# Six of the queries' column tiles as three pairs by seven products, the pair operands of h made while v is multiplied, and attention's result by way of DRAM

## The chip, the cores and the metric

The kernel runs on one core of one Trainium2 chip. The metric is the device time of that core in microseconds, lower is better. PE is TensorE's matmul queue, PEld its weight loads; DVE is VectorE, ACT is ScalarE, POOL is GpSimd and SP is SyncE, which issues most DMAs.

## What is computed

One trunk layer of a decoder, for 512 prompt tokens and 64 sample tokens together (576 columns), with a width of 1024. Cut from the reference:

```python
h = _rmsnorm(x, norm1_g) * (1.0 + sc1) + sh1          # sc1, sh1, g1, ...: silu(c) @ w_ada + b_ada
proj = h @ w_in                                       # 1024 x 6656
b_gate, c_gate, xa, q, k, v, ga, gb = jnp.split(proj, cuts, axis=-1)
uc, new_conv = _causal_conv(c_gate * xa, conv_buf, conv_w)
ya = (b_gate * uc) @ w_conv_out
o, k_state, v_state = attend(q, k, v, sinks)          # window 128, 16 heads of 64, 4 kv heads
yb = o @ w_attn_out
mixed = jax.nn.sigmoid(ga) * ya + jax.nn.sigmoid(gb) * yb
x = x + g1 * (mixed @ w_mix_out)
# then a ConvFFN (w_up, depthwise convolution, GELU gate, w_down) in the same manner, and a final norm
```

The results are wanted in float32. Every matrix product is made from high and low parts: three passes, weights high by activations high, high by low, low by high.

## The kernel before, in words

Activations lie transposed: eight row blocks of 128 channels by 576 tokens, each as a high and a low tile. A weight block of 1024 rows by 128 columns is loaded by SP (`raw`), its high part made by ACT (`whi`), its low part by DVE (`wlo`). There are four buffers for `raw` and five each for `whi` and `wlo`.

`product(w, xs)` makes one column tile of 128: eight k-steps of three passes in two column groups (256 and 320), 48 matmuls. `pair_product` makes two column tiles by seven products of half the size (Strassen's manner): each of seven parts is four k-steps of three passes of 288 columns, 12 matmuls, 84 in all. Its weights are sums of the two tiles' blocks (`pair_weights`: A, B and C of 1024 columns, D of 512, made by four DVE sums of 512 and then split); its activations are sums and differences of blocks of h (`PairOperands`: four DVE sums of 288 columns for each of four block pairs, a high part on ACT, a low part on DVE). The seven parts go into three PSUM banks X, Y and Z. Between parts ACT subtracts one bank from another (`minus`) or copies one; the outputs are read by the functions `out_a0` to `out_b1`.

In order of the program: norm and modulation up to about 50 us; v as five products of another shape (`for i in range(5)`, 53 to 67 us); the first two tiles of the queries (67 to 73); then the loop `for at, m in enumerate(PLAIN)` with six turns, to about 228. Each turn makes column tile m of c and of x of the convolution branch by two plain products. Turns 1, 2 and 3 also make a part of the keys (`key_parts`) and two tiles of the queries (`queries`), by plain products. In turns 4 and 5 of before, the pair operands of h are made. Then come 14 pair jobs with w_in, 4 pair jobs with w_conv_out (the last ends at about 450), 8 plain products with w_attn_out (450 to 497), the mix, and the ConvFFN.

`queries` splits each tile into q and a low part and copies half of it between partitions by POOL-issued DMAs (`q<-low`). Attention's scores, softmax and values run as a generator beside all this: `tick()`, called after each k-step, advances it by a rate, `filler[1]`. After attention the same generator runs `modulation`, which loads tiles of w_ada (`ada<-in_w_ada` on SP) and multiplies them (`side_by_side`, L1234). Attention's result o is kept in two tiles `ot` of tag "oh" until `part_o` splits it during the last pair jobs.

PE's order is the program's from attention on, and the jobs also fix that of ACT and DVE. In the PLAIN loop a scheduler sets the order on ACT, DVE, POOL and SP. The helpers record their operations at one line, L112 (before) and L114 (after), so tiles are told apart by name.

Of the kernel before, what the change touches and what calls it, by code (L numbers as in the profile page):

```python
# [16 lines left out]
P = 128  # L17
# [13 lines left out]
ROWS_AHEAD = 5  # L31
PLAIN = (0, 1, 2, 4, 5, 6)
Q_TICKS = 8
CACHE_AT = 15, 16
EPS = 1e-6
NEG = -1e33
# [36 lines left out]
def step_kernel(ctx: ExitStack, tc: tile.TileContext, ins: dict, outs: list):  # L73
# [169 lines left out]
    class PairOperands:  # L243
# [47 lines left out]
        def all(self):  # L291
# [2 lines left out]
            self.low()  # L294
            self.n3()

    class BesideOperands:


# [91 lines left out]
            self.low(self.x1, self.r1)  # L391
            self.low(self.n4, self.r0[:, :HT])

    def pair_weights(ra, rb, moved=""):
# [22 lines left out]
        def s3_slots():  # L417
            return slot("wh", F32R, [P, 4, P]), slot("wl", F32R, [P, 4, P])
# [30 lines left out]
    def pair_product(w, x, steps, out_a0, out_a1, out_b0, out_b1):  # L449

        X, Z = (aux()[:, :HT] for _ in range(2))
        Y = halves(mmps())[1][:, :HT]
        p5 = slot("p5")[:, :HT]

        def part(bank, wn, xn_, more=True):

            (hi, lo), xs = w[wn], x[xn_]
            for k in range(4):  # L460
                xh, xl = xs[k]
                passes = (hi(k), xh), (hi(k), xl), (lo(k), xh)
                for n, (wt, xx) in enumerate(passes):
# [345 lines left out]
    for j in (2, 0, 1):  # L809
# [2 lines left out]
            nc.scalar.activation(t[:, c0:c1], x, AF.Copy, scale=HD**-0.5 if j == 2 else 1.0)  # L812
        kT.append(t)
    q0 = kT.pop(0)

    def state_load(src, n):

# [25 lines left out]
    def tok_cols(t, i):  # L843

        at = i * P if i < 4 else NT - P
        return t[:, at : at + P]

    for i in range(5):
        ps = aux()
        for k in range(NK):  # L850
            whi, wlo = (x[:, k % 4, :] for x in wv[k // 4])
# [32 lines left out]
            nc.gpsimd.dma_start(x[other].bitcast(F32), x[mine].bitcast(F32))  # L884
        KS[hd] = kh, kl

    def queries(t, ps=None):

        scale = HD**-0.5 if ps is None else 1.0
# [32 lines left out]
        nc.gpsimd.dma_start(snk, ins["attn_sinks"][0, :].partition_broadcast(P))  # L922
    )
    key_parts(0)
    queries(0, q0)
    queries(1)
    con = slot("con", shape=[P, 520])
    nc.sync.dma_start(con[:, 0:256], ins["consts"][:, CND : CND + 256])
    nd = con[:, 0:256]
# [36 lines left out]


    pinned.append(pe)
    ot = [wp.tile([P, 4, NT], F32, tag="oh", name=nm("o"), bufs=2) for _ in range(2)]

    def softmax_steps(s, n, sinks, nsinks, w):

# [83 lines left out]
    def decode_values(q, s, cV):  # L1056
# [9 lines left out]
            pt.append(t)  # L1066
            yield False
        yield False
        c = slice(512 + 32 * q, 512 + 32 * q + 32)
        for j in range(2):  # L1070
            O = aux()
            parts = [(vt(4)[:, j * P : j * P + P], pt[1], slice(0, P))]
# [9 lines left out]
            oX = slot("oX", shape=[P, 2, 32])  # L1082
            for hf in range(2):
                src = O[HALF[hf], :P].rearrange("p (b x g t) -> p x g b t", b=4, x=2, g=2)
                dst = ot[j][:, 2 * hf : 2 * hf + 2, c]
# [44 lines left out]

    def prompt_values(parts):
        O = aux()
        for u, (hd, i, pts) in enumerate(parts):
            nkt, c = len(pts), slice(256 * u, 256 * u + 256)
            for n in range(2 * nkt):
# [7 lines left out]
                if u + n:  # L1143
                    tc.keep_in_program_order(done)
        for u, (hd, i, pts) in enumerate(parts):
            nc.scalar.copy(
                ot[hd // 2][:, 2 * (hd % 2) : 2 * (hd % 2) + 2, i * P : i * P + P],
                O[:, 256 * u : 256 * u + 256].rearrange("p (g c) -> p g c", g=2),
            )

    def attention():
        units = [(hd, i) for hd in range(4) for i in range(4)]
# [17 lines left out]
        for n in range(3):  # L1170
# [3 lines left out]
            if before is not None:  # L1174
                yield from before
            before = decode_values(n, s, more)

    sto = cp.tile([P, 18 * NF], F32, tag="sto", name="sto")

# [98 lines left out]

    def beside_conv():
        yield from attention()  # L1280
        filler[1] = 40 / 84
        yield from modulation(2048)
        yield True

    fill(beside_conv(), .3)
    sg_dram = dp.tile([2, NK, P, NT], F32, name="sg_dram")
    ycv, gcv, made, made_g = {}, {}, {}, {}
    wco, wao = ins["w_conv_out"][0], ins["w_attn_out"][0]

    class Job:  # L1290
# [7 lines left out]
            self.raws = [load_w(kpm(self.mat, self.c + e), NK) for e in (0, self.apart)]  # L1298

        def prepare(self, moved="", late=False):  # L1300
            self.w, t = pair_weights(*self.raws, moved=moved)
# [122 lines left out]
    hp = [PairOperands(h, kp, made, xn) for kp in range(4)]  # L1424

    def operands(kp):
        hp[kp].sums()
        hp[kp].high()
        hp[kp].low()

    for at, m in enumerate(PLAIN):
        if at in (4, 5):
# [6 lines left out]
                    ),  # L1439
                )  # L1440
            )
        if 1 <= at <= 3:
            key_parts(at)
            for t in (2 * at, 2 * at + 1):
                queries(t)
        w = weights(kpm(w_in, 1024 + m * P), NK)
        if at in (4, 5):
            operands(2 * at - 8)
        if at == 5 and filler:
            filler[1] = .4  # L1450
        ps = product(w, h)
# [6 lines left out]
        c_sb = slot("c")  # L1458
        nc.scalar.copy(c_sb, ps)
        w = weights(kpm(w_in, 2048 + m * P), NK)  # L1460
        if at in (4, 5):
            operands(2 * at - 7)
        steps = {}
        if at == len(PLAIN) - 1:
            jobs[0].load()
        if at == len(PLAIN) - 1:
# [24 lines left out]
    def g_list(names):  # L1491
        return [g_at(int(n[0]), n[1:]) for n in names.split()]

    jobs[0].before = {2: [op.n3 for op in hp]}
    jobs[1].before = {3: [lambda: inner[6]()]}
    jobs[7].before = {2: [lambda: inner[3]()]}
    jobs[8].before = {2: [lambda: inner[7]()]}
# [8 lines left out]
        },  # L1506
        12: {0: "1third_low 3third 2third_low", 2: "3third_low"},
    }
    for n, at in plan.items():
        jobs[n + 2].after = {p: g_list(names) for p, names in at.items()}  # L1510
    for n in range(4):
        if n:
            jobs[n_conv + n].before = {
                1: [lambda n=n: late[2 * n - 2]()], 2: [lambda n=n: late[2 * n - 1]()],
            }
    jobs[-1].after = {
        2: [lambda: part_o(2)], 3: [lambda: part_o(3)],
        4: [lambda: w_next.update({1: split_w(w_raw)})], 5: [lambda: part_o(4)], 6: [lambda: part_o(6)],
        7: [lambda: part_o(8)],
    }  # L1520

    def part_o(n):
        for k in range(len(o), n):
            o.append(split_slot(ot[k // 4][:, k % 4, :], "o"))

    for n, job in enumerate(jobs):
        if n + 1 == len(jobs):
# [711 lines left out]
```

## Time and profile before

| | before |
|---|---|
| time, median of 3 runs | 962.78 us (962.68 to 963.0) |
| profiled execution | 963.13 us, of which span 961.0 |
| PE busy | 946.4 us, 98% of the span, 7326 matmuls |
| DVE, ACT, POOL busy | 711.9, 539.1, 132.3 us |
| moved by DMA | 144.08 MB, mean 150 GB/s |

The profile is of one execution; its busy times are shares of the span. Windows of the trace give the same for a stretch of time; groups of instructions give a count, the busy time and the mean of one; the waits give what an engine waited for, in total, how often, and the longest.

### The profile page before, as it was taken

How to read it: one execution, taken by the hardware profiler on the slowest of the kernel's cores; microseconds unless marked ns; L12 is line 12 of the kernel's file. 1: busy time of each engine (PE TensorE's matmuls, PEld its weight loads, DVE VectorE, ACT ScalarE, POOL GpSimd, SP SyncE). 2: the span in 40 equal slices, each digit the busy share in tenths (PEclk: the TensorE clock that was granted, in tenths of full speed). 3: DMA queues.
4: the chain of work that ended last, by engine and by line, in shares of the span. 5: the costliest groups of instructions: out<-in, count | busy, mean ns of one | idle time of the engine just before them, and what ended most of it. 6: DMA issues, size and time to landing. Idle time of an engine off the chain costs nothing.

```text
span 961.0 us, 18726 instructions
## 1 busy us (share of the span) xinstructions
PE 946.4 (98%) x7326; PEld 912.7 (95%) x7326; DVE 711.9 (74%) x1331; ACT 539.1 (56%) x1020; POOL 132.3 (14%) x309
## 2 busy tenths in 40 slices
PE   6999999999999999999999999999999999999997
PEld 5799999998999989999889999999999999999997
DVE  4656787697966767776677688995559998868874
ACT  5454665556665446875335567563226565546664
POOL 2122112201211011210001131100000001101110
PEclk9999999999999999999999999999999999999999
DMA  9985332423655767899885732332323333328542
GB/s 275 330 255 147 90 86 71 131 90 96 155 147 178 244 219 199 219 250 285 283 291 119 174 97 66 89 109 67 107 88 92 89 89 101 92 72 172 138 95 99
DMA packets 182650, 144.08 MB, mean 150 GB/s; under 512 B 7688, under 2 KB 162124, under 8 KB 182274
## 3 DMA queue, kind: packets, MB, share of 16 engines
q1 hardware_dynamic: 172546, 111.72, 38.8%
q0 software_dynamic: 9872, 30.92, 14.0%
q8 instruction: 57, 0.93, 0.4%
q14 instruction: 31, 0.25, 0.1%
q10 hardware_dynamic: 144, 0.26, 0.1%
HBM read 113.89 MB, written 12.07 MB: 131 GB/s over the span
## 4 chain that ended last, share of the span: by engine, by line
PE 95%; DMA 3%; SPq 1%; ACT 0%; DVE 0%; issue 0%; DVEq 0%
PE mm L112 55%; PE aux L112 37%; PE aux L1234 2%; DMA ad<-in_w_ada 1%; PE aux L1137 1%; DMA raw<-in_w_in 1%; SPq L497 1%; DMA q<-low 0%; ACT whi L112 0%; ACT wlo L112 0%; DVE cs L504 0%; ACT hh L112 0%; DVE hl L112 0%; DVE yo L112 0%; ACT acc L112 0%
## 5 line engine op out<-in xcount | busy, mean ns | idle before, releaser
L112 ACT ACTIVATE whi<-raw 128x1024 fp32r<-128x1024 f32 (+3 forms) x183 | 185.6, 1022 | 108.7 <-PE mm L112 51.9
L112 DVE TENSOR_TENSOR wlo<-raw,whi 128x1024 fp32r<-128x1024 f32 (+2 forms) x160 | 188.8, 1186 | 49.0 <-ACT whi L112 48.1
L112 PE MATMUL mm<-hh,whi 128*128 128x256 f32 x336 | 74.3, 302 | 0.5 <-ACT hh L112 0.5
L112 PE MATMUL mm<-hh,wlo 128*128 128x256 f32 x336 | 71.7, 295 | 0.0
L112 PE MATMUL mm<-hl,whi 128*128 128x256 f32 x336 | 70.8, 295 | 0.1
L112 PE MATMUL aux<-2h,whi 128*128 128x288 f32 (+2 forms) x232 | 68.6, 296 | 0.0
L112 PE MATMUL aux<-2l,whi 128*128 128x288 f32 (+2 forms) x232 | 68.5, 295 | 0.0
L112 PE MATMUL aux<-2h,wlo 128*128 128x288 f32 (+2 forms) x232 | 68.3, 294 | 0.0
L112 DVE TENSOR_TENSOR raw<-raw 128x512 f32<-128x512 f32 x82 | 57.5, 701 | 2.6
L112 PEld LDWEIGHTS mm<-hh,whi 128*128 128x128 f32 x336 | 55.1, 189 | 1.8 <-ACT hh L112 1.0
L112 PEld LDWEIGHTS mm<-hl,whi 128*128 128x128 f32 x336 | 55.6, 188 | 0.7 <-DVE hl L112 0.5
L112 PEld LDWEIGHTS mm<-hh,wlo 128*128 128x128 f32 x336 | 56.2, 188 | 0.0
L112 PE MATMUL aux<-hh,whi 128*128 128x288 f32 (+2 forms) x184 | 54.0, 301 | 0.0
L112 PE MATMUL aux<-hl,whi 128*128 128x288 f32 (+2 forms) x184 | 53.0, 295 | 0.0
L112 PE MATMUL aux<-hh,wlo 128*128 128x288 f32 (+2 forms) x184 | 52.9, 295 | 0.0
L112 PE MATMUL mm<-th,whi 128*128 128x288 f32 x164 | 49.2, 300 | 0.0
L112 PE MATMUL mm<-nh,whi 128*128 128x288 f32 x164 | 49.0, 299 | 0.0
L112 PE MATMUL mm<-th,wlo 128*128 128x288 f32 x164 | 48.6, 296 | 0.0
L112 PE MATMUL aux<-th,wlo 128*128 128x288 f32 x164 | 48.5, 296 | 0.0
L112 PE MATMUL aux<-th,whi 128*128 128x288 f32 x164 | 48.5, 296 | 0.0
L112 PE MATMUL mm<-nh,wlo 128*128 128x288 f32 x164 | 48.5, 296 | 0.0
L112 PE MATMUL mm<-nl,whi 128*128 128x288 f32 x164 | 48.4, 295 | 0.0
(374 smaller groups left out, 3012.3 us busy)
## 6 DMA issues: line engine op xcount, KB each, us to landing
raw<-in_w_in SPq DMA_DIRECT2D x52, 512.0 KB, 5.0
raw<-in_w_up SPq DMA_DIRECT2D x44, 512.0 KB, 3.8
ada<-in_w_ada SPq DMA_DIRECT2D x64, 256.0 KB, 5.5
wlo<-raw POOLq DMA_DIRECT2D x17, 512.0 KB, 4.6
ad<-in_w_ada SPq DMA_DIRECT2D x32, 256.0 KB, 6.6
raw<-in_w_down SPq DMA_DIRECT2D x16, 512.0 KB, 4.2
sg_dram<-sg POOLq DMA_DIRECT2D x16, 288.0 KB, 4.9
gt<-sg_dram SPq DMA_DIRECT2D x16, 288.0 KB, 6.0
```

What stands on the lines that cost most here:

```text
L112: done = getattr(self.engine, name)(*args, **kwargs)
L497: return tc.keep_in_program_order(nc.sync.dma_start(dst, src))
L1137: done = nc.tensor.matmul(O[HALF[par], c], vt(i - nkt + 1 + kt)[:, hd * 64 : hd * 64 + 64], pts[kt][:, par * 256 : par * 256 + 256], start ...
L1234: done = nc.tensor.matmul(ps[32 * j : 32 * j + 32, :], cT[:, k, :], cols[k][j], start=(k == 1), stop=(k == NK - 2),)
```

## The change

At turns 1, 2 and 3 of the PLAIN loop (`Q_PAIRS`), the two tiles of the queries are made by one `pair_product` instead of two plain products. Its weights are prepared during the plain product ahead of it (`q_job`), D in a `whi` and a `wlo` tile instead of slots of their own (`narrow=False`). X and Y lie in the banks of the plain products and Z in a small one (`apart=True`). The result goes to SBUF (`qt`), and `queries` reads it there.

The pair operands of h are made during v's product (`EarlyOperands`, one block pair at each of i = 1 to 4) and not at turns 4 and 5; n3, which was made in jobs[0], is made with them. They take the two "oh" tiles. So o lies in slots `ot`, is written to `o_dram` by POOL-issued DMAs (eight of 128x512 and one for the 64 sample columns), and is read back by `load_o` on SP, eight loads of 128x576, in the last two pair jobs.

Besides: the copies of o from PSUM are 32 of 128 columns and not 16 of 256; the mask constants `nd` lie in a part of V; the table load of Exp stands earlier; the filler's rate is .2 in a pair and .32 after it; the rate of the modulation goes from 40/84 to 40/100; and some of the last operands ("third") for w_conv_out's jobs stand one part earlier.

```diff
+Q_PAIRS = (1,2,3,)
+OPS_AT = 1, 2, 3, 4
...
+    class EarlyOperands(PairOperands):
+        def high(self):
+            made, (h0, l0), (h1, l1) = self.made, *self.x
+            if "t" not in made:
+                made["t"] = [wp.tile([P, 4, NT], F32R, tag="oh", name=nm("t"), bufs=2) for _ in range(2)]
+            self.th, self.tl = (x[:, self.kp, :] for x in made["t"])
+            act.activation(self.th, self.t, AF.Copy)
...
+            act.activation(self.nh, self.r[0][:, a], AF.Copy)
+            act.activation(self.n3h, self.r[0][:, b], AF.Copy)
...
+        def low(self):
+            for lo, src, hi in (
+                (self.tl, self.t, self.th), (self.nl, self.r[0][:, :HT], self.nh),
+                (self.n3l, self.r[0][:, HT:], self.n3h),
+            ):
+                dve.tensor_tensor(out=lo, in0=src, in1=hi.bitcast(F32), op=ALU.subtract)
...
-        X, Z = (aux()[:, :HT] for _ in range(2))
-        Y = halves(mmps())[1][:, :HT]
+        X, Y = (halves(mmps())[1][:, :HT] if apart or n else aux()[:, :HT] for n in range(2))
+        Z = aux()[:, :HT]
...
+    act.activation(first, q0[:, 0:1], AF.Exp, scale=0.0)
...
     for i in range(5):
+        if i in OPS_AT:
+            EarlyOperands(h, OPS_AT.index(i), made, xn).all_early()
...
-    ot = [wp.tile([P, 4, NT], F32, tag="oh", name=nm("o"), bufs=2) for _ in range(2)]
+    ot = []
+    o_dram = dp.tile([NK, P, NT], F32, name="o_dram")
+    od = []
...
-            nc.scalar.copy(
-                ot[hd // 2][:, 2 * (hd % 2) : 2 * (hd % 2) + 2, i * P : i * P + P],
-                O[:, 256 * u : 256 * u + 256].rearrange("p (g c) -> p g c", g=2),
-            )
+            for g in range(2):
+                at = 256 * u + P * g
+                t = ot[2 * hd + g]
+                nc.scalar.copy(t[:, i * P : i * P + P], O[:, at : at + P])
+                if i == 3:
+                    nc.gpsimd.dma_start(o_dram[2 * hd + g, :, 0:512], t[:, 0:512])
...
-        filler[1] = 40 / 84
+        filler[1] = 40/100
...
     for at, m in enumerate(PLAIN):
+        w = weights(kpm(w_in, 1024 + m * P), NK)
         if 1 <= at <= 3:
             key_parts(at)
-            for t in (2 * at, 2 * at + 1):
-                queries(t)
-        w = weights(kpm(w_in, 1024 + m * P), NK)
-        if at in (4, 5):
-            operands(2 * at - 8)
+            if at in Q_PAIRS:
+                qt = [slot("qt") for _ in range(2)]
+                filler[1] = .2
+                pair_product(q_job.w, made["op"], {}, *copy_outs(qt), True)
+                filler[1] = .32
+            for n in range(2):
+                queries(2 * at + n, qt[n] if at in Q_PAIRS else None)
...
         w = weights(kpm(w_in, 2048 + m * P), NK)
-        if at in (4, 5):
-            operands(2 * at - 7)
         steps = {}
+        if at + 1 in Q_PAIRS:
+            q_job = Job(w_in, Q0 + (2 * at + 2) * P, None, None)
+            q_job.load()
+            fs = [f for x in q_job.prepare("").values() for f in x]
+            for k, n in [(0, 2), (1, 1), (2, 1), (3, 1), (4, 2), (5, 1), (6, 1), (7, 1)]:
+                steps[k], fs = fs[:n], fs[n:]
...
-    jobs[0].before = {2: [op.n3 for op in hp]}
...
+    jobs[-2].after = {4: [lambda: load_o(2)], 6: [lambda: load_o(4)]}
     jobs[-1].after = {
-        2: [lambda: part_o(2)], 3: [lambda: part_o(3)],
+        0: [lambda: load_o(5)], 1: [lambda: load_o(6)],
+        2: [lambda: part_o(2), lambda: load_o(7)], 3: [lambda: part_o(3), lambda: load_o(8)],
...
+    def load_o(n):
+        for k in range(len(o) + len(o_raw), n):
+            o_raw.append(slot("ot"))
+            nc.sync.dma_start(o_raw[-1], o_dram[k])
```

On ACT, at the start of turn 1, before has the weights' high parts and the queries' copies one after the other (`whi` a weight block, `y` the convolution, `kh` the keys, `s` an exp of the softmax):

```order
L112 ACTIVATE whi_1588<-raw_1586 128x1024
L112 ACTIVATE y_1096<-pad_1089,parT 128x592
L112 ACTIVATE kh_1100<-kT_663 64x512
L112 ACTIVATE whi_1702<-raw_1700 128x1024
L896 ACTIVATE q_1230<-mm_1112 64x512
L896 ACTIVATE q_1231<-mm_1112 64x512
L984 ACTIVATE s_1119,den_1139<-s_1119,nmx_1135 128x256 x2
```

The same place on ACT in after:

```order
L114 ACTIVATE whi_1180<-raw_1178 128x1024
L114 ACTIVATE y_1174<-pad_1167,parT 128x592
L114 ACTIVATE kh_1184<-kT_663 64x512
L1029 ACTIVATE s_1092,den_1112<-s_1092,nmx_1108 128x128 x2
L1029 ACTIVATE s_1093,den_1112<-s_1093,nmx_1108 128x128 x2
L114 ACTIVATE mm_1193<-mm_1192 128x288
L1035 ACTIVATE es_1113<-es_1113 128x4
L114 COPY p_1195<-aux_1194 128x288
L114 ACTIVATE aux_1194<-mm_1193 128x288
```

The pair's steps between its parts (`mm_1193<-mm_1192`, the copy `p_1195`, `aux_1194<-mm_1193`) now stand in ACT's queue behind a plain weight's high part, y, kh and the exps.

On SP, around the last pair job, before has the loads of w_attn_out, of gates (`gt`) and of w_ada:

```order
L151 DMA raw_5625<-in_w_attn_out 128x8x128
L1365 DMA gt_5627<-sg_dram 128x576
L1365 DMA gt_5629<-sg_dram 128x576
L1250 DMA ada_5641<-in_w_ada 128x512
L1250 DMA ada_5657<-in_w_ada 128x512
L151 DMA raw_5791<-in_w_attn_out 128x8x128
```

The same place on SP in after:

```order
L153 DMA raw_5700<-in_w_attn_out 128x8x128
L1585 DMA ot_5675<-o_dram 128x576
L1585 DMA ot_5677<-o_dram 128x576
L1417 DMA gt_5702<-sg_dram 128x576
L1417 DMA gt_5704<-sg_dram 128x576
L1585 DMA ot_5712<-o_dram 128x576
L1302 DMA ada_5718<-in_w_ada 128x512
L1585 DMA ot_5731<-o_dram 128x576
L1302 DMA ada_5736<-in_w_ada 128x512
L153 DMA raw_5874<-in_w_attn_out 128x8x128
```

The loads of o now stand between those of the weights, the gates and w_ada.

On POOL, before has the queries' copies of a head group in a row:

```order
L903 DMA q_1690<-low_1689 64x512
L903 DMA q_1691<-low_1689 64x512
L903 DMA q_1822<-low_1821 64x512
L903 DMA q_1823<-low_1821 64x512
L914 DMA qS_830<-qX_831 64x4x16 x2
```

After has writes of o among them:

```order
L947 DMA q_1832<-low_1831 64x512
L947 DMA q_1833<-low_1831 64x512
L947 DMA q_1843<-low_1842 64x512
L1200 DMA o_dram<-ot_1587 128x512
L1200 DMA o_dram<-ot_1588 128x512
L947 DMA q_1844<-low_1842 64x512
```

Two writes of o stand ahead of the group's last copy.

More of the change, by code (lines that the diff above doesn't have):

```diff
@@ L295, in all, with all_early @@
             self.n3()
+    class EarlyOperands(PairOperands):
[5 more added lines that the diff above has]
+            act.activation(self.th, self.t, AF.Copy)
+            if self.kp % 2 == 0:
+                for n in ("n4", "n3"):
+                    made[n] = slot(n + "h", F32R), slot(n + "l", F32R)
+            a, b = slice(0, HT), slice(HT, NT)
+            at = (a, b)[self.kp % 2]
+            nh, nl = made["n4"]
+            self.nh, self.nl = nh[:, at], nl[:, at]
+            self.n3h, self.n3l = (x[:, at] for x in made["n3"])
+            act.activation(self.nh, self.r[0][:, a], AF.Copy)
+            act.activation(self.n3h, self.r[0][:, b], AF.Copy)
+            for name, hi, lo, c in (
+                ("x00", h0, l0, a), ("n3", *made["n3"], at), ("x10", h1, l1, a), ("x11", h1, l1, b),
+                ("n1", self.th, self.tl, a), ("t2", self.th, self.tl, b), ("n4", nh, nl, at),
+            ):
+                made.setdefault("op", {}).setdefault(name, []).append((hi[:, c], lo[:, c]))
+        def all_early(self):
+            self.sums()
+            self.high()
+            self.low()
+        def low(self):
+            for lo, src, hi in (
+                (self.tl, self.t, self.th), (self.nl, self.r[0][:, :HT], self.nh),
+                (self.n3l, self.r[0][:, HT:], self.n3h),
+            ):
+                dve.tensor_tensor(out=lo, in0=src, in1=hi.bitcast(F32), op=ALU.subtract)
     class BesideOperands:
@@ L392, in third_low, with pair_weights @@
             self.low(self.n4, self.r0[:, :HT])
-    def pair_weights(ra, rb, moved=""):
+    def pair_weights(ra, rb, moved="", narrow=True):
         c0, c1 = slice(0, 4), slice(4, 8)
@@ L417, in s3_slots @@
         def s3_slots():
+            if not narrow:
+                return [x[:, 0:4, :] for x in tiles()]
             return slot("wh", F32R, [P, 4, P]), slot("wl", F32R, [P, 4, P])
@@ L447, in in_turn, with pair_product @@
         return {at: (lambda names=names: [t[n]() for n in names.split()]) for at, names in order.items()}
-    def pair_product(w, x, steps, out_a0, out_a1, out_b0, out_b1):
-        X, Z = (aux()[:, :HT] for _ in range(2))
-        Y = halves(mmps())[1][:, :HT]
+    def pair_product(w, x, steps, out_a0, out_a1, out_b0, out_b1, apart=False):
+        X, Y = (halves(mmps())[1][:, :HT] if apart or n else aux()[:, :HT] for n in range(2))
+        Z = aux()[:, :HT]
         p5 = slot("p5")[:, :HT]
@@ L846, in tok_cols @@
         return t[:, at : at + P]
+    made = {}
     for i in range(5):
+        if i in OPS_AT:
+            EarlyOperands(h, OPS_AT.index(i), made, xn).all_early()
         ps = aux()
@@ L885, in key_parts, with queries @@
         KS[hd] = kh, kl
-    def queries(t, ps=None):
-        scale = HD**-0.5 if ps is None else 1.0
+    def queries(t, ps=None, scale=HD**-0.5):
         if ps is None:
@@ L924, in step_kernel @@
     key_parts(0)
-    queries(0, q0)
+    queries(0, q0, 1.0)
     queries(1)
-    con = slot("con", shape=[P, 520])
-    nc.sync.dma_start(con[:, 0:256], ins["consts"][:, CND : CND + 256])
-    nd = con[:, 0:256]
+    nd = V[2][:, 1, :]
+    nc.sync.dma_start(nd, ins["consts"][:, CND : CND + 256])
     con2 = slot("con2", shape=[P, 520])
@@ L1068, in decode_values @@
         yield False
-        c = slice(512 + 32 * q, 512 + 32 * q + 32)
+        c = slice(32 * q, 32 * q + 32)
+        if not od:
+            od.append(slot("od", shape=[P, NK, 64]))
         for j in range(2):
@@ L1132, in prompt_values @@
         O = aux()
+        while len(ot) < 2 * parts[-1][0] + 2:
+            ot.append(slot("ot"))
         for u, (hd, i, pts) in enumerate(parts):
@@ L1176, in attention @@
             before = decode_values(n, s, more)
+        nc.gpsimd.dma_start(o_dram[:, :, 512:576].rearrange("k p c -> p k c"), od[0])
     sto = cp.tile([P, 18 * NF], F32, tag="sto", name="sto")
@@ L1286, in step_kernel @@
     sg_dram = dp.tile([2, NK, P, NT], F32, name="sg_dram")
-    ycv, gcv, made, made_g = {}, {}, {}, {}
+    ycv, gcv, made_g = {}, {}, {}
     wco, wao = ins["w_conv_out"][0], ins["w_attn_out"][0]
@@ L1300, in prepare @@
         def prepare(self, moved="", late=False):
-            self.w, t = pair_weights(*self.raws, moved=moved)
+            self.w, t = pair_weights(*self.raws, moved=moved, narrow=self.outs is not None)
             order = {0: "sums1 ah al", 1: "bh bl", 3: "dh dl sums2", 4: "ch", 5: "cl"}
@@ L1422, in step_kernel @@
     jobs += [Job(wco, m * P, made_g, lambda m=m: conv_outs(m)) for m in range(0, NK, 2)]
[L1424 to L1429, printed above, removed]
     for at, m in enumerate(PLAIN):
```

7 lines of the change are left out of this document (4 added, 3 removed), and 2 rows, old and new, of the table plan.

## The prediction

> **What bounds the kernel now.** First the page's head, the shares of the chain that ended last, then the waits of PE.
>
> ```profile
> span 961.0 us, 18726 instructions
> PE 946.4 (98%) x7326; PEld 912.7 (95%) x7326; DVE 711.9 (74%) x1331; ACT 539.1 (56%) x1020; POOL 132.3 (14%) x309
> PE 95%; DMA 3%; SPq 1%; ACT 0%; DVE 0%; issue 0%; DVEq 0%
> ```
>
> ```profile
> PE aux L112 <- POOL ident masks.py:199: 4.4, 1, 4.4
> PE aux L112 <- DMA q<-low: 0.3, 1, 0.3
> ```
>
> PE is busy in 98% of the span and is 95% of the chain. Its longest wait is the start's 4.4 us; the only one inside the queries' stretch is 0.3 us, for a query's copied half. So a matmul taken off PE is worth its duration unless it uncovers something. The next two rows of the chain give the price of matmuls by kind.
>
> ```profile
> 199.05 3.17 PE mm L112 x24
> 302.47 1.59 PE aux L112 x12
> ```
>
> A plain product is 48 matmuls, two such rows. One of a pair's seven parts is 12 matmuls of 288 columns, one row of the second kind (1.59; 1.595 as the mean of such rows). The windows below give, for each stretch, its length and the busy time of PE, PEld, DVE, ACT and POOL, then granted clock, DMA share and GB/s: v's product, the first queries with the plain product after them, the three stages that get a pair, then the stretch of w_attn_out in which o is to be loaded.
>
> ```profile
> 56.00:67.00 11.00, 11.00 (x95) 11.00 (x95) 1.62 (x2) 3.63 (x8) 0.54 (x1) 1.00 0.94 259
> 67.00:89.00 22.00, 22.00 (x172) 22.00 (x170) 12.62 (x34) 11.56 (x24) 8.27 (x17) 1.00 0.60 167
> 89.00:122.80 33.80, 33.80 (x266) 33.06 (x265) 28.70 (x80) 19.96 (x55) 5.85 (x12) 1.00 0.33 88
> 122.80:156.50 33.70, 33.70 (x266) 31.97 (x265) 24.52 (x68) 20.83 (x58) 4.91 (x12) 1.00 0.34 88
> 156.50:192.40 35.90, 35.58 (x280) 33.75 (x280) 26.93 (x75) 20.81 (x58) 7.42 (x13) 1.00 0.38 110
> 430.00:440.00 10.00, 10.00 (x78) 10.00 (x77) 5.84 (x8) 6.36 (x10) 1.71 (x2) 1.00 0.87 210
> 440.00:450.00 10.00, 10.00 (x77) 9.86 (x76) 6.40 (x9) 7.33 (x13) 0.00 (x0) 1.00 1.07 324
> 450.00:460.00 10.00, 10.00 (x77) 9.71 (x80) 7.82 (x11) 2.72 (x6) 0.00 (x0) 1.00 1.04 363
> 460.00:470.00 10.00, 10.00 (x80) 8.69 (x73) 4.57 (x6) 2.14 (x3) 0.00 (x0) 1.00 1.08 353
> 470.00:480.00 10.00, 10.00 (x79) 8.40 (x78) 8.73 (x13) 5.86 (x7) 0.00 (x0) 1.00 0.53 173
> ```
>
> PE is full in all of them at clock 1.00. DVE has 5 to 9 us free in a stage of 34, and the DMA engines have nothing free from 440 to 470.
>
> **The pairs: what PE saves.** Two plain products are 4 x 3.17 = 12.68 us; a pair is 7 x 1.595 = 11.165. That is 1.515 us a pair, **4.55 us** for three. All other matmuls stay.
>
> **The pairs: what DVE and ACT get.** The groups by shape, DVE and then ACT:
>
> ```profile
> L112 DVE TENSOR_TENSOR wlo<-raw,whi 128x1024 fp32r<-128x1024 f32 x150 | 182.7, 1222 | 47.7 <-ACT whi L112 46.8
> L112 DVE TENSOR_TENSOR raw<-raw,raw 128x512 f32<-128x512 f32 x41 | 28.2, 688 | 0.1
> L112 DVE TENSOR_TENSOR wl<-s,wh 128x512 fp32r<-128x512 f32 x25 | 17.3, 694 | 13.6 <-ACT wh L112 13.6
> L112 DVE TENSOR_TENSOR tl<-tw,th 128x576 fp32r<-128x576 f32 x20 | 15.1, 753 | 4.0 <-ACT th L112 3.8
> L112 DVE TENSOR_TENSOR xn<-xn,xn 128x288 f32<-128x288 f32 x4 | 1.8, 452 | 0.0
> ```
>
> ```profile
> L112 ACT ACTIVATE whi<-raw 128x1024 fp32r<-128x1024 f32 x167 | 175.3, 1056 | 103.2 <-PE mm L112 46.4 <-DVE raw L112 35.1 <-issue 6.2
> L112 ACT ACTIVATE mm<-aux 128x288 f32<-128x288 f32 x41 | 16.3, 398 | 34.5 <-PE aux L112 34.5
> L984 ACT ACTIVATE s<-s,nmx 128x128 f32<-128x128 f32 x16 | 6.2, 391 | 3.6 <-DVE nmx L978 3.4 <-ACT pt L1127 0.2
> L112 ACT ACTIVATE y<-pad,parT 128x592 f32<-128x592 f32 x8 | 6.3, 788 | 7.7 <-POOL sto L1211 6.0 <-DVE pad L112 1.6
> L112 ACT ACTIVATE kh<-kT 64x512 fp32r<-64x512 f32 x4 | 2.5, 628 | 0.0
> L112 ACT ACTIVATE th<-tw 128x576 fp32r<-128x576 f32 x20 | 13.6, 680 | 14.5 <-DVE tw L112 13.6 <-PE aux L112 0.9
> L112 ACT ACTIVATE nh<-xn 128x288 fp32r<-128x288 f32 x4 | 1.7, 430 | 0.0
> L1146 ACT COPY o<-aux 128x256 f32<-128x256 f32 x16 | 5.2, 375 | 9.5 <-PE aux L1137 9.5
> ```
>
> A pair splits three blocks of 1024 and one of 512 where two plain products split two of 1024. DVE thus gets 4 sums x .688, one 1024 low more (1.222), one 512 low (.694) and two output sums (2 x .452, from the row of that size): 5.53 us a pair. In the first pair stage, 89 to 122.8, that makes 28.70 + 5.53 = 34.2 against PE's 33.8 - 1.5 = 32.3. The 1.9 us over must be carried into the next stage, where 24.52 + 5.53 + 1.9 = 32.0 just fits 32.2; the third has 26.93 of 34.4 plus little. I take it as carried, because low halves are made a product ahead of their use, and the last stage has slack: **0**. If that cover goes, it is the third rival.
>
> On ACT the pair's chain stands in a fixed order: at the pair's start the high half of the next plain weight comes first (its tile comes free only when the product ahead ends), then y, kh, four exps, and only then the Z - Y step (the PSUM copy) that part 3 needs: 1.056 + .788 + .628 + 4 x .391 + .398 = 4.43 us. Cover on PE: parts 1 and 2 and the eight scores matmuls between them, in the timeline of PE of before
>
> ```profile
> 82.34 0.22 PE L112 MATMUL aux<-kh,q 128*128 128x128 f32 x1
> ...
> 83.18 0.49 PE L112 MATMUL mm<-hh,whi 128*128 128x256 f32 x2
> ```
>
> 0.84 from the first of them to the next product. 2 x 1.595 + .84 = 4.03: PE stalls 0.4. This order holds for pairs 1 and 2; at pair 3 the exps stand ahead of the plain weight. **+0.8** in all; the bounds are 0 (exps done earlier) and 1.6 (part of y late as well).
>
> **The operands beside v.** Four times DVE: four sums of .452, a low of .753, two of .452, 3.47 us, 13.9 in all; ACT .680 + 2 x .430, 6.2 in all. From 56 to 89 DVE is idle 9.4 + 9.4 us and ACT 7.4 + 10.4. No pair reads them before the first pair, at about 89. **0**, bound +1 if h's last low halves slip behind them. They issue no DMA; n3, which jobs[0] made in its part 2, comes along and is counted in the 3.47. The work that leaves at = 4, 5 and jobs[0] only lengthens idle time there, since PE was full: 0. The pairs' four weight loads a stage are the same four loads as before, asked for one product earlier at a DMA share of .33: 0.
>
> **o by way of DRAM.** The copies become 32 of 128 columns: at most 32 x .375 = 12.0 us for 6.0 on ACT, a lane with 13 us free per stage: 0. The reloads are another matter. SP's timeline, then the issue of the eighth ada tile of this stretch and its landing, then the group of matmuls that reads it:
>
> ```profile
> 428.96 9.88 SPq L151 DMA_DIRECT2D raw<-in_w_attn_out  x2
> ```
>
> ```profile
> L1250 SPq DMA_DIRECT2D ada<-in_w_ada x1: 541/541/541, 450.1 to 450.1; - x1
> DMA to landing us min/median/max: 6.5/6.5/6.5
> ```
>
> ```profile
> 459.71 1.92 PE L1234 MATMUL aux<-ada,cT 128*32 128x512 f32 x16
> ```
>
> ```profile
> gt<-sg_dram SPq DMA_DIRECT2D x16, 288.0 KB, 6.0
> ```
>
> Six of the eight loads (288 KB each, as gt) stand on SP behind the second of those two raw loads (issued by 438.8) and ahead of that ada tile: 1.77 MB. At the mean of 324 and 363 GB/s this is 5.15 us of a stretch that has no free time. Free are: the tile's own slack, 459.71 - (450.1 + 6.5) = 3.1, and half a microsecond at the end of 430 to 440, where the rate was still 210. So 5.15 - 3.1 - .5 = **+1.5** on PE at L1234; bounds 0 (the loads start earlier) and 2.05 (no half microsecond). Behind the loads on SP stand the next raw loads and the later ada tiles; those have the 10 us from 470, where the rate was 173, to catch up: 0. The other two loads go out ahead of that raw load, where the rate was 210: 0. The last two land a microsecond or two after ACT could split them, but PE reads those blocks in the last two of eight k-steps of w_attn_out's first product, .79 us each (a quarter of 3.17) and so 4.7 us after its first: 0, bound +.5. The rows show 324 to 363 GB/s when all is busy. The Trainium skill, "DMA: Bandwidth & Descriptors", Specifications, gives a ceiling of about 435 GB/s for the fabric and about 358 for HBM per core: by 435, an estimate from that page, the six loads take 4.1 us, the stall is 0.5 and the sum a microsecond lower; the trace agrees with the lower figure, its best 10 us stand at 363.
>
> **Queues.** POOL issues o_dram's writes between the queries' copies. One issue, in POOL's timeline:
>
> ```profile
> 145.44 0.52 POOL L903 DMA_DIRECT2D q<-low  x1 [10.27 <-DVE low L899]
> ```
>
> Two writes ahead of the last copy of head groups 2 and 3 are 1.04 us later each, plus what ACT's copy is late. The scores read it a whole product later, and before's margin ended in the 0.3 us wait above: I take **0**, bound 2 x 1.04. The earlier table load and the slower ada rate move work inside idle time; the thirds of the plan moved one part ahead: 0, bound +.5.
>
> **Sum.** -4.55 + .8 + 1.5 = -2.25. The profiled execution took 963.13 (span 961.0 and 2.1 around it), 0.35 over the median of 962.78. So 960.9 for such an execution and **960.5** as the median.
>
> **The rivals.**
> 1. *All covers hold.* -4.55: **958.2**. For it: PE waits for almost nothing now, and loads could start in the free part of 430 to 440. Against: the ACT order is fixed. 0.15.
> 2. *No change.* The reloads cost their upper bound and both late copies are waited for: -4.55 + .8 + 2.05 + 2.1 = +.4: **963.2**. For it: the saturated rows, the existing wait for q. Against: a product lies between copy and scores. 0.22.
> 3. *Slower: DVE sets the pace of the pair stages.* DVE's waits from 89 to 192.4 hold this row:
>
> ```profile
> DVE den L991 <- ACT es L990: 8.8, 7, 1.7
> ```
>
> If DVE stands in order at such waits (2.9 us a stage) while the pair's sums queue behind, the first stage needs 34.2 + 2.9 = 37.1 against 32.3, +4.8, and the second 24.52 + 5.53 + 2.9 = 33.0 against 32.2, +.8. Then -4.55 + 5.6 + .8 + 1.5 = +3.35: **966.1**. It decides once the first stage's overhang is more than the weights' lead, one product of 6.3 us. The Trainium skill, "PSUM — Partial Sum Buffer", Engine vs sequencer instructions, calls the queues of VectorE and ScalarE strictly FIFO: by it a waiting den holds the sums behind it, as the seven waits do. Against: 34.2 is less than 1 us over with waits filled by other work. 0.19.
>
> **How the numbers follow.** The forecast has 0.44; its own range is 958.2 to 961.6 (bounds of the ACT chain, the reloads, the plan). No change means within 0.2%, 1.9 us, about what a measurement of this kernel can tell. Of the forecast .38 lies below 960.9, with rival 1 .53 faster; .06 and rival 2 make .28; rival 3 .19. The range goes from 957.8 (rival 1 less 0.4) to 965.0: it leaves out most of rival 3 and a little at the low end.
>
> **What would show it.** Right: PE's matmuls down by 36, pair parts of 1.59 at mm/aux, a PE wait of about .4 for ACT at the first two pairs, one of 1 to 2 us for ada at L1234 of before. Wrong: PE waits for DVE between 89 and 192 (rival 3), for DMA q (rival 2), none at all (rival 1); and any wait elsewhere, in h's operands or in the jobs' third steps.

## The result, and the profile after

The changed kernel takes 965.92 us (median of 14 runs, 963.83 to 969.31) against 962.94 us (14 runs, 961.69 to 964.24): the ratio is 1.0031, 95% interval 1.0019 to 1.0044. It is slower by 3.0 us where 2.2 us faster was forecast.

The profiled execution took 969.21 us, near the upper end, so its waits are probably larger than those of a usual run; the sizes of the causes are taken from the medians of the experiments. Its page, as before's:

```profile
span 967.4 us, 18745 instructions
PE 947.5 (98%) x7290; PEld 910.1 (94%) x7290; DVE 725.5 (75%) x1355; ACT 549.7 (57%) x1058; POOL 137.5 (14%) x318
PE 89%; DMA 7%; issue 2%; ACT 1%; DVE 1%; POOL 0%; SPq 0%; POOLq 0%; ACTq 0%
```

There are 36 matmuls fewer, as there should be, and yet PE is busy 1.1 us longer; and 7% of the chain is now DMA, where it was 3%. The waits of PE name the DMA:

```profile
PE aux L1286 <- DMA ada<-in_w_ada: 4.9, 2, 2.9
PE mm L114 <- ACT mm L114: 0.3, 1, 0.3
```

L1286 is `side_by_side`, the modulation's matmuls (L1234 before), which waited for nothing in before. The second row is the pair's ACT chain. The two waits for w_ada, and three for o's parts, in PE's timeline:

```profile
380.87 2.96 PE L1286 MATMUL aux<-ada,cT 128*32 128x512 f32 x16 [2.92 <-DMA ada<-in_w_ada]
...
458.77 0.53 PE L114 MATMUL mm<-oh,whi 128*128 128x256 f32 x2 [0.33 <-ACT oh L114]
459.57 0.53 PE L114 MATMUL mm<-ol,whi 128*128 128x256 f32 x2 [0.27 <-DVE ol L114]
461.02 0.54 PE L114 MATMUL mm<-ol,whi 128*128 128x256 f32 x2 [0.26 <-DVE ol L114]
465.37 1.92 PE L1286 MATMUL aux<-ada,cT 128*32 128x512 f32 x16 [1.95 <-DMA ada<-in_w_ada]
```

The first of these waits belongs to the last group of the first modulation. The same 16 matmuls take 2.96 us there and 1.92 at 465.37. The windows around it (length, PE, PEld, DVE, ACT, POOL, granted clock as a share of the full one, DMA share, GB/s) say why, the last of them between the borders of the slow stretch:

```profile
378.00:381.00 3.00, 0.14 (x4) 0.14 (x8) 2.56 (x5) 0.16 (x1) 0.00 (x0) 1.00 0.75 142
381.00:384.00 3.00, 3.00 (x17) 0.62 (x13) 0.00 (x0) 0.00 (x0) 0.00 (x0) 0.60 0.56 167
384.00:387.00 3.00, 3.00 (x20) 3.00 (x21) 0.00 (x0) 0.78 (x3) 0.07 (x1) 0.83 0.69 186
381.70:385.00 3.30, 3.30 (x17) 1.47 (x10) 0.00 (x0) 0.00 (x0) 0.00 (x0) 0.50 0.83 241
```

After the wait the granted clock is 0.60 and then 0.83: 3 x 0.40 + 3 x 0.17 = 1.7 us more, which shows as busy time. These are means over three microseconds each; the last row shows the clock itself, 0.50, so the slow stretch is some 3.4 us long (1.7 / 0.5). What that group waited for stands in the timelines of SP and POOL:

```profile
367.62 2.41 SPq L1302 DMA_DIRECT2D ada<-in_w_ada  x3
```

```profile
369.16 1.14 POOL L114 DMA_DIRECT2D sg_dram<-sg  x2 [3.99 <-ACT sg L114]
372.99 0.91 POOL L114 DMA_DIRECT2D wlo<-raw  x1 [2.69 <-ACT p L114]
375.18 0.87 POOL L114 DMA_DIRECT2D wl<-s  x1 [1.28 <-ACT wl L114]
```

At the slower rate the last tiles are asked for at 367 to 370, among a pair job's gate writes and moved weight halves; the last landed 11 us later. In before the last of them went out at 360.4. That the gate writes and weight halves are what slows them is an inference from the time; the rate's part in it is tested below.

There is a third cause, with no wait at all. Attention's value matmuls (`aux<-pt,V`, 64 weight columns each), first before's timeline, then after's at the same place:

```profile
130.20 1.95 PE L1137 MATMUL aux<-pt,V 128*64 128x256 f32 x16
132.08 0.66 PE L112 MATMUL aux<-ident,s 128*128 128x128 f32 x4
```

```profile
131.20 1.94 PE L1186 MATMUL aux<-pt,V 128*64 128x256 f32 x14
133.07 0.40 PE L114 MATMUL mm<-n4h,whi 128*128 128x288 f32 x1
...
136.44 0.65 PE L1186 MATMUL aux<-pt,V 128*64 128x256 f32 x2
137.02 0.66 PE L114 MATMUL aux<-ident,s 128*128 128x128 f32 x4
```

Sixteen together take 1.88 us from their start to the next start. Torn into 14 and 2 they take 1.87 and 0.58: two matmuls of a pair that are not neighbours no longer run side by side. The 14 are six pairs, whose matmuls start 0.007 us apart, and two single ones; each single one takes as long as a pair, 0.22 us. Four groups are torn so, three at 0.57 us and one at 0.14: 1.85. PE's order shows it (the last two of a group and what stands between them):

```
862 L1186 MATMUL aux_1868<-pt_1746,V_685 64x256
863 L114 MATMUL mm_1655<-n4h_721,whi_1518 128x288 [waits DVE_49]
...
886 L114 MATMUL mm_1855<-hh_352,wlo_1643 128x320
887 L1186 MATMUL aux_1868<-pt_1746,V_685 64x256
```

### The profile page after: what moved, and what is told of

It reads as the page before. It is cut to its first block, busy times and chain, and to the rows that moved or that the text cites. A ratio compares the mean times of both kernels' runs of the same rounds, so it can differ in the third digit from the quotient of the medians.

```text
span 967.4 us, 18745 instructions
## 1 busy us (share of the span) xinstructions
PE 947.5 (98%) x7290; PEld 910.1 (94%) x7290; DVE 725.5 (75%) x1355; ACT 549.7 (57%) x1058; POOL 137.5 (14%) x318
## 4 chain that ended last, share of the span: by engine, by line
PE 89%; DMA 7%; issue 2%; ACT 1%; DVE 1%; POOL 0%; SPq 0%; POOLq 0%; ACTq 0%
PE mm L114 49%; PE aux L114 37%; DMA ad<-in_w_ada 2%; DMA ada<-in_w_ada 2%; PE aux L1286 2%; PE aux L1186 2%; DMA ot<-o_dram 1%; DMA raw<-in_w_in 1%; DMA wlo<-raw 1%; DMA raw<-in_w_down 1%; DMA x<-in_x_prompt 0%; ACT whi L114 0%; SPq L538 0%; ACT s L1029 0%; DVE wlo L114 0%
## 5 line engine op out<-in xcount | busy, mean ns | idle before, releaser
L114 PE MATMUL mm<-hh,whi 128*128 128x256 f32 (+2 forms) x264 | 60.7, 303 | 0.5 <-ACT hh L114 0.5
L114 PE MATMUL mm<-hh,wlo 128*128 128x256 f32 (+2 forms) x264 | 58.3, 295 | 0.0
L114 PE MATMUL aux<-hh,whi 128*128 128x288 f32 (+1 forms) x196 | 57.4, 300 | 0.0
L114 PE MATMUL mm<-hl,whi 128*128 128x256 f32 (+2 forms) x264 | 57.4, 295 | 0.0
L114 PE MATMUL aux<-hl,whi 128*128 128x288 f32 (+1 forms) x196 | 56.4, 294 | 0.0
L114 PE MATMUL aux<-hh,wlo 128*128 128x288 f32 (+1 forms) x196 | 56.4, 294 | 0.0
L114 PE MATMUL mm<-fh,whi 128*128 128x256 f32 x224 | 47.9, 295 | 0.5 <-DVE rt L114 0.5
L114 PE MATMUL mm<-fl,whi 128*128 128x256 f32 x224 | 47.8, 295 | 0.0
L114 PE MATMUL mm<-fh,wlo 128*128 128x256 f32 x224 | 47.8, 295 | 0.0
L114 PEld LDWEIGHTS aux<-2l,whi 128*128 128x128 f32 x232 | 43.7, 188 | 0.0
```

The lines of the kernel that those rows point to most:

```text
L114: done = getattr(self.engine, name)(*args, **kwargs)
```

## The experiments

Theory A after the result: three separate causes, torn value groups, the later end of the first modulation, and o's reloads ahead of the second modulation's tiles. Its rivals are named with each run. "Before" was run beside each set: 962.93, 962.65 and 962.94 us.

**The rate alone.**

```diff
-        filler[1] = 40/100
+        filler[1] = 40/84
```

> The changed kernel with the modulation's rate set back to 40/84, nothing else. Theory A (the last modulation group, moved later, asks for its w_ada tiles in the burst of the jobs' moved weight halves; PE waits 2.9 us and then runs at a low granted clock): no wait at the side_by_side line near 380, and 2 to 4.7 us less than the changed kernel's 965.9, so 961.2 to 963.9. Rival (the loss sits in the pair stages or in run-to-run clock, whatever the rate): 965.9, within 0.7.

Measured: 964.82 us (8 runs), 1.1 less than the changed kernel and between the two cases. The wait near 380 is gone (timeline of PE of this run), and the one after 450 is left:

```profile
371.82 1.92 PE L1286 MATMUL aux<-ada,cT 128*32 128x512 f32 x16
...
461.23 2.54 PE L1286 MATMUL aux<-ada,cT 128*32 128x512 f32 x16 [2.14 <-DMA ada<-in_w_ada]
```

The wait goes with the slower rate, but not always: the four profiled runs at 40/100 show it with 2.92 (the changed kernel), 2.05, 0.82 and, without pairs, 0 us; none at 40/84 has it. So the 2 to 4.7 us that one profiled run suggested were too much. The size of 1.1 is itself uncertain: the intervals against before, 1.0010 to 1.0031 here and 1.0019 to 1.0044 for the changed kernel, overlap.

**Value matmuls kept together.**

```diff
-                if u + n:
-                    tc.keep_in_program_order(done)
+                tc.keep_in_program_order(done)
```

> The changed kernel with every value matmul of attention kept in program order, the first of a group too, so that no group is torn apart by product matmuls. Theory A (two value matmuls of 64 weight columns run side by side only when adjacent; the four torn groups cost 1.8 us): the values' share of PE time falls from 16.2 to 14.4 us and the time by 1.8, to 964.1. Rival (the lost time only shows there and is made up by waits elsewhere): 965.9, within 0.7.

Measured: 963.99 us (12 runs), 1.9 less; the intervals overlap here too (1.0003 to 1.0027), but the trace gives 1.85 by itself. None of its eight groups is torn, and the one shown takes 1.88 us again:

```profile
136.32 1.95 PE L1186 MATMUL aux<-pt,V 128*64 128x256 f32 x16
138.20 0.66 PE L114 MATMUL aux<-ident,s 128*128 128x128 f32 x4
```

Without pairs no group is torn (the fourth run below has before's order there), so the pairs bring this cost with them, by way of the scheduler. Why it delays the last matmul of a group whose first is free to move was not found.

**Six reloads of o taken away.**

```diff
-            nc.sync.dma_start(o_raw[-1], o_dram[k])
+            if k < 2:
+                nc.sync.dma_start(o_raw[-1], o_dram[k])
+            else:
+                nc.gpsimd.memset(o_raw[-1], 0.0)
```

> The changed kernel with six of the eight reloads of o replaced by memsets on POOL (o's blocks 2 to 7 are zero); the writes to DRAM stay. Theory A (1.77 MB on SP ahead of the w_ada tiles delay them and o itself): the waits at the first modulation group after 450 and for oh and ol go, 2.8 to 3.8 us, so 962.1 to 963.1. Rival (the group waits for other loads of that stretch, w_attn_out and the gates): 965.9, within 0.7.

This run leaves o's blocks 2 to 7 at zero. Measured: 961.68 us (12 runs), 4.2 less, a little over the upper end and clear of the changed kernel (0.9983 to 1.0003). PE's timeline has no wait for w_ada after 450, and none for o:

```profile
457.64 1.92 PE L1286 MATMUL aux<-ada,cT 128*32 128x512 f32 x16
```

**No pairs.**

```diff
-Q_PAIRS = (1,2,3,)
+Q_PAIRS = ()
```

> The changed kernel with no pairs (the six tiles by plain products again; early operands, o by way of DRAM and the rate stay). Theory A (pairs are worth 4.55 less 0.4 of stall, less 1.8 of torn value groups, so 2.2): 968.1. Rival (VectorE sets the pace in the pair stages, as the third rival of the prediction had it): the pairs cost 3 us or more there, and the time falls to 963 or less.

Measured: 968.54 us (6 runs). The pairs are worth 2.6 us as they stand, near 4.55 less the 1.9 of torn groups. The rival falls. The size is rough: this run has no wait near 380, and waits for queries that the changed kernel doesn't have:

```profile
PE aux L114 <- DMA q<-low: 1.2, 2, 0.9
```

**The traffic alone, in the kernel before.** Eight loads at just the places of o's reloads:

```diff
+    def more(*ks):
+        for k in ks:
+            nc.sync.dma_start(slot("xt"), sg_dram[0, k])
+
+    jobs[-2].after = {4: [lambda: more(0, 1)], 6: [lambda: more(2, 3)]}
     jobs[-1].after = {
+        0: [lambda: more(4)], 1: [lambda: more(5)],
-        2: [lambda: part_o(2)], 3: [lambda: part_o(3)],
+        2: [lambda: part_o(2), lambda: more(6)], 3: [lambda: part_o(3), lambda: more(7)],
```

> The kernel before with eight more loads of 288 KB (gates from DRAM, not used by anything) at just the places on SP where the changed kernel reloads o. Theory A (the traffic ahead of the w_ada tiles is the cost, whatever it is for): a wait of 2 to 3 us at the first modulation group after 450 and about 3 us more than before: 965.2 to 966.9. Rival (only o itself, read late by ACT, costs): no more than 0.5, so 963.4 or less.

Measured: 965.33 us (6 runs), 2.7 us more than before by the medians; the ratio of 1.0040 (1.0026 to 1.0055) would be 3.9. Nobody reads these tiles; the waits of PE of this run name the w_ada tiles behind them, and the second view is of the eighth of these tiles, the last that the group needs:

```profile
PE aux L1234 <- DMA ada<-in_w_ada: 2.2, 1, 2.2
```

```profile
L1250 SPq DMA_DIRECT2D ada<-in_w_ada x1: 328/328/328, 454.9 to 454.9; - x1
DMA to landing us min/median/max: 6.6/6.6/6.6
```

So 2.7 us or more of the 4.2 is traffic ahead of the w_ada tiles (eight loads here, six in the run without reloads). The rest, 1.5 at most, is put down to o itself being late, which no run shows alone: three waits of 0.86 in the timeline above, each worth some 0.2 more than it shows (matmuls of this form last 0.27 but follow each other every 0.13, and that overlap is lost at a wait).

**All three edits.** The diffs of the first three runs together.

> The changed kernel with three edits at once: rate 40/84, value matmuls kept together, six reloads of o replaced by memsets (o's blocks 2 to 7 are zero). Theory A (three separate causes that add up: 1.1, 1.9 and 4.2 by the medians of the single edits): 965.9 - 7.2 = 958.7, about what the pairs alone should give, 962.9 - 4.55 + 0.4 = 958.8. Rival (they overlap, one wait taking the place of another): 960.5 to 961.7.

Measured: 958.16 us (5 runs), ratio 0.9957 (0.9945 to 0.9969), where the sum of the single edits gives 958.7. Page and a window of this run:

```profile
PE 941.9 (98%) x7290; PEld 907.8 (95%) x7290; DVE 726.2 (76%) x1355; ACT 549.2 (57%) x1058; POOL 138.2 (14%) x324
```

```profile
450.00:460.00 10.00, 10.00 (x78) 8.40 (x77) 5.16 (x7) 1.63 (x2) 0.00 (x0) 1.00 1.08 370
```

This run, too, leaves o's blocks 2 to 7 at zero. PE is busy 4.5 us less than in before, at full stretch also where the changed kernel waited. Of the 4.5, 0.6 lies ahead of the first product, where before's clock fell for a while and this run's didn't; from there on it is 927.3 and 923.4 us, 3.9 less. The three causes add up, and nothing else of a size that these runs can tell is left.

**Ways out, the second modulation first.** Rate 40/84 and values kept, as in all runs from here on, and

```diff
-            fill(modulations(1), 0.6)
+            fill(modulations(1), 0.5)
```

> Nothing left out: rate 40/84, values kept together, and the second modulation at a rate of 0.5 for 0.6, so that its tiles are asked for more slowly beside o's reloads. Theory A (DMA bandwidth in 440 to 480 is the cost; the demand of the w_ada tiles falls from about 300 to 250 GB/s): most of the 2 to 2.7 us wait at the first group goes, o's splits stay late by 0.8: 960 to 961.5. Rival (the first group still asks for its tiles at the same place on SP behind o's reloads): 962.9, what the two first edits alone give (965.9 - 3.0).

Measured: 965.76 us (5 runs); a miss. The wait for w_ada fell to 0.4 us, but the modulation no longer ends before `drain()` (it runs what the generator has left) behind w_attn_out, which then issues the rest at once. Waits and windows of this run:

```profile
PE aux L114 <- ACT row L1308: 4.2, 1, 4.2
```

```profile
500.00:510.00 10.00, 6.44 (x51) 4.76 (x49) 6.59 (x11) 3.35 (x5) 0.86 (x1) 1.00 0.92 223
510.00:520.00 10.00, 9.37 (x60) 9.37 (x61) 2.20 (x6) 0.58 (x2) 0.00 (x0) 0.83 0.00 1
```

**The second modulation one job earlier.**

```diff
-        if n + 1 == len(jobs):
+        if n + 2 == len(jobs):
             drain()
-            fill(modulations(1), 0.6)
+            fill(modulations(1), 0.4)
```

> Nothing left out: rate 40/84, values kept together, and the second modulation begun one pair job earlier at a rate of 0.4, so that the same w_ada tiles are spread over 120 steps of PE and not 77. Theory A (bandwidth): no wait for w_ada over 0.5 us, o late by less than 0.8: 959.5 to 961. Rival (the moved weight halves of the last jobs fill 410 to 440, and the tiles collide with those instead): 962 to 963.5.

Measured: 969.23 us (5 runs); a miss, worse than either case. The same forced end is there (4.2 us for `row`), and 1.2 us for w_ada besides. Neither theory had the forced end in it.

**Two edits, the reloads left as they are.**

> Nothing left out: rate 40/84 and values kept together, the reloads of o as in the changed kernel. Theory A (three causes that add up): 965.9 - 1.1 - 1.9 = 962.9, with a wait of 2 to 2.7 us for w_ada at the first group after 450 and about 0.8 for o's splits as what is left. Rival (once the two are gone the first group comes earlier on PE and its tiles do not, so the wait grows by what was saved ahead of it): 964 to 965, a wait of 4 us.

Measured: 962.68 us (12 runs), ratio 0.9993 (0.9981 to 1.0005): the sum again, and no different from before. So the two edits together are clear of the changed kernel, which neither is alone. PE's timeline has what is left:

```profile
458.60 1.92 PE L1285 MATMUL aux<-ada,cT 128*32 128x512 f32 x16 [1.82 <-DMA ada<-in_w_ada]
```

**Reloads earlier.**

```diff
-    jobs[-2].after = {4: [lambda: load_o(2)], 6: [lambda: load_o(4)]}
+    jobs[-2].after = {2: [lambda: load_o(2)], 3: [lambda: load_o(4)], 4: [lambda: load_o(6)]}
     jobs[-1].after = {
-        0: [lambda: load_o(5)], 1: [lambda: load_o(6)],
-        2: [lambda: part_o(2), lambda: load_o(7)], 3: [lambda: part_o(3), lambda: load_o(8)],
+        0: [lambda: load_o(7)], 1: [lambda: load_o(8)],
+        2: [lambda: part_o(2)], 3: [lambda: part_o(3)],
```

> Rate 40/84, values kept together, and six of o's reloads asked for one pair job earlier, ahead of the w_attn_out load on which SP stands idle from 434 to 442. Theory A (bandwidth from 440 on is the cost, and 430 to 440 has some to spare): four transfers fewer in the full stretch, 3.4 us of its traffic, so the wait for w_ada falls below 0.5 us and o's splits are not late: 958.5 to 960.5. Rival (no slot is free for them that early, SP waits in order and the weights behind come late): 963 or more.

Measured: 962.27 us (11 runs), ratio 0.9986 (0.9977 to 0.9995); between the cases. Six loads did go out by 428, and no wait for o is left, but the group still waits, in PE's timeline and the window around it:

```profile
457.30 2.86 PE L1285 MATMUL aux<-ada,cT 128*32 128x512 f32 x16 [2.27 <-DMA ada<-in_w_ada]
```

```profile
450.00:460.00 10.00, 7.74 (x55) 5.30 (x53) 3.77 (x5) 0.31 (x1) 0.00 (x0) 0.91 1.07 375
```

The stretch is full at 375 GB/s without most of o: the tiles of w_ada, the weights and the gates fill it. (A group needs 8 tiles of 256 KB, and the groups are 14 us apart, so w_ada's mean demand is 150 GB/s; the 300 in the expectation for the rate of 0.5 is twice that.) The wait did not shrink because PE gets there 1.8 us earlier than in the run ahead (455.0 against 456.8), and the last of the 8 tiles lands only 1.3 earlier (457.3 against 458.6): it goes out 2.5 us earlier but is on its way for 8.3 us and not 7.1. Why it takes longer stays open.

**A slower second modulation with a later end.**

```diff
-            fill(modulations(1), 0.6)
+            fill(modulations(1), 0.5)
...
-    drain()
-    affine(A2, 32, 56, NK)
...
     residual(product(w_mix0, mixed), x1[0], 16)
+    drain()
+    affine(A2, 32, 56, NK)
```

> Rate 40/84, values kept together, the second modulation at 0.5 and its end no longer forced after w_attn_out but after the first product of the mix. Theory A (the rate of 0.5 had taken away the wait at the first group, and its 4.2 us wait for the modulation's row was the forced end alone): 965.8 - 4.2 - 0.5 of low clock behind it, 960 to 961.5. Rival (the wait only moves to the new end): 964 to 966.

Measured: 960.58 us (7 runs), ratio 0.9969 (0.9958 to 0.9980). It takes 5.2 us less than with the forced end; that end was the whole loss of the rate of 0.5.

```profile
459.40 1.92 PE L1285 MATMUL aux<-ada,cT 128*32 128x512 f32 x16 [0.86 <-DMA ada<-in_w_ada]
```

**Both.** The diffs of the two runs above.

> The edits of the two runs ahead of this together: rate 40/84, values kept together, six of o's reloads earlier, second modulation at 0.5 with its end after the first product of the mix. Theory A (both act on the same traffic, so the gains don't add): 958.2 to 959.5, the level of the run without six reloads, 958.2. Rival (one of the two moves its wait elsewhere): 961 or more.

Measured: 959.79 us (6 runs), ratio 0.9969 (0.9956 to 0.9981), a little above the theory's range and not told apart from the run above it. PE's timeline and a window:

```profile
458.29 1.92 PE L1285 MATMUL aux<-ada,cT 128*32 128x512 f32 x16
```

```profile
450.00:460.00 10.00, 10.00 (x80) 8.54 (x78) 4.71 (x7) 1.63 (x2) 0.00 (x0) 1.00 1.07 366
```

These two versions compute the whole result and beat both kernels, before by 0.3%.

## Why the prediction was wrong, point by point

| step | forecast | shown |
|---|---|---|
| matmuls saved by the pairs | -4.55 | PE busy 3.9 to 4.5 less with the three causes away; 2.6 net of the torn groups |
| ACT chain in pairs 1 and 2 | +0.8 | one wait of 0.3 at pair 1, none at pair 2 |
| o's reloads | +1.5, at most 2.05 | +4.2: 2.7 or more of it traffic, the rest put down to o's last blocks |
| slower modulation rate | 0 | +1.1 |
| value groups torn | not in the sum | +1.9 |

With the ACT wait at 0.4 (0.3 and the lost overlap) and the saving as forecast the terms make -4.55 + 0.4 + 4.2 + 1.1 + 1.9 = +3.05; the measured difference is +2.98. That they meet so closely is luck, since each of the sizes from medians can be off by a microsecond or more.

- **The saving was right in the main**, and so was the cover of the pairs' sums and of the operands beside v: PE waits for no DVE from 50 to 200. The third rival (DVE sets the pace) did not come. In the first pair stage DVE has 30.1 of 32.3 us, not 34.2 (the terms of a pair on DVE add up to 5.57 us and not to the 5.53 used, on which nothing hangs), and its wait for den fell from 8.8 us in seven to 1.9 in two; DVE's windows and waits of after:

```profile
86.40:118.70 32.30, 31.99 (x250) 31.02 (x249) 30.12 (x81) 23.39 (x65) 6.16 (x12) 1.00 0.34 91
```

```profile
DVE den L1036 <- ACT es L1035: 1.9, 2, 1.7
```

- **The query copies** cost nothing, as forecast; the second rival's 2.1 us for them did not come.
- **The reloads' step failed by its bounds.** Place and mechanism were as described. With the traffic put into before, the eighth tile lands at 461.5, 4.9 us later than before's 456.6 (the sum has 5.15 less 0.5), and PE waits 2.2 for it, so most of the slack was free as forecast; in the changed kernel PE waits 1.95. But the median of that run is 2.7 more, over the upper bound of 2.05; what costs the difference is not shown. And "0, bound +.5" for o's last blocks was up to 1.5: ACT and DVE had them split too late for three of PE's reads.
- **"The slower ada rate moves work inside idle time" is the step that has no working behind it.** It was put at 0 without asking what the last tiles would meet on the DMA queues 9 us later; the runs put it at 1.1, roughly.
- **The torn groups were in PE's order, which had been read for the pair parts alone.** The sum took "all other matmuls stay": their number stays, their neighbours don't. By the Trainium skill, "TensorEngine Tiling (Array Packing)", Tiling Modes, a matmul of 64 weight columns takes one of two tiles of the array, and two such can run at once; the trace agrees (0.12 us each in a whole group, 0.29 torn).

Of the named rivals only the second had a part of the slower outcome, the reloads at their upper bound; that the third's figure, 966.1, is near the measured one is chance. The range was too narrow at the top: it allowed for one full DMA stretch and not for a second, and for no cost in matmuls that the change doesn't touch.

## What to carry to other kernels

- When PE bounds, the saving is the sure part of the sum; the rest is to be looked for in the loads that the change makes later or adds, each against the rate of the very 10 us in which it will run, and at the place where a wait is forced (a drain, a first use).
- Read the changed order for the instructions that the change does not touch, too: here a matmul of half the array's width took as long alone as a pair of them together, 0.22 us.
- A median of single edits sizes a cause; one profile shows its place. Here the same wait was 2.9 us in one profile and worth 1.1 in the median, and with some ten runs that vary by 4 to 7 us even the median can be off by a microsecond.

## What was not expected of the hardware

A wait of PE can cost twice. In six of the profiled runs the granted clock fell in mid-kernel, 0.8 to 1.3 us after PE went on: behind waits of 2.05 (values kept together), 2.14 (rate alone), 2.27 (reloads earlier), 2.92 (the changed kernel) and twice 4.2 us (the rate of 0.5, one job earlier). Each time it was 0.50 for some 3.4 us, so 1.7 us of full speed were lost whatever the wait; 0.83 or 0.91 in a window of 10 us is the mean with the rest at 1.00. After waits of 2.68 (values kept together, the second one) and 2.2 us (the loads in before) it stayed at 1.00, and from 25 us to the kernel's last microseconds no shorter wait had a fall behind it. At the start shorter ones did: in five runs the clock fell during or behind a wait of 1.4 to 1.9 us near 15 us, and in others with such a wait it didn't. Before's start, in the columns of the windows above, follows a wait of 1.86:

```profile
17.80:21.00 3.20, 3.20 (x30) 1.50 (x23) 1.43 (x2) 0.35 (x2) 0.00 (x0) 0.50 1.12 327
```

The Trainium skill, "TensorE: Matmul & The Clock Gate", Why this matters for your kernels, asks for no idle gap over about 3 us between bursts of matmuls; here gaps from 2.05 us on, and at the start from 1.4, could already lower the clock, though not each time.
